# Loading the second matrix of a batched product by pairs of batches, with 16 KB in one piece per partition

## The chip, the cores and the metric

One core of one Trainium2 chip. The metric is the device time of one execution in microseconds (us), the median of several. The "span" is the part of it that the profile covers, from the first recorded event to the last. Differences here are a few tenths of a microsecond, so most kernels were run five or six times in turn with the kernel before, on the same chip. The sessions used different chips (5, 10, 8 and 0), so kernels of different sessions are compared by their ratios to the kernel before.

## The reference

```python
batch, m, k, n = 16, 512, 512, 512
a: float32 [batch, k, m];  b: float32 [batch, n, k]
out = np.matmul(a.transpose(0, 2, 1), b.transpose(0, 2, 1)).astype(np.float32)
```

For each batch the product contracts over k. The kernel gives TensorE its operands with k on the partitions: a has it there when its rows are loaded, b does not and is transposed first.

## The kernel before

SyncE loads one batch of b and one of a, 1 MiB each, into four buffers each. VectorE casts b to bfloat16, TensorE transposes it (two bfloat16 values travel as one float32), VectorE copies the result out of PSUM. ScalarE casts a. TensorE multiplies in two halves of eight matmuls; VectorE copies out the first half and ScalarE the second. Stores go out by pairs of batches, 2 MiB each: five from ScalarE's queue, the last three from SyncE after the loads.

```python
LOADS = 4; OUTS = 5; LAG = 3; TAIL = 3; H = B // 2
b_v = b.rearrange("b (ni no) k -> b ni no k", no=NO)      # NO = 4: 8 KB a partition
b_sb = [sb(f"b_sb{s}", [P, NO, K], f32) for s in range(LOADS)]
b_bf = [sb(f"b_bf{s}", [P, NO, K], cdt) for s in range(2)]
bt_ps = [ps(f"bt_ps{s}", [P, KJ, NO, P], f32) for s in range(2)]
# ... (cut)
def run_sp(sp):
    for i in range(B):
        s, use = i % LOADS, i // LOADS
        if use:
            sp.wait_ge(turned, i - LOADS + 1)
        sp.dma_start(b_sb[s][:], b_v[i]).then_inc(b_in[s], 16)
        if use:
            sp.wait_ge(summed, MO * (i - LOADS) + 1)
        if i % 2 == 0 and i // 2 >= OUTS:
            sp.wait_ge(o_out[i // 2 % OUTS], 16 * (i // 2 // OUTS))
        sp.dma_start(a_sb[s][:], a_v[i]).then_inc(a_in[s], 16)
    for j in range(H - TAIL, H - 1):
        sp.wait_ge(summed, MO * (2 * j + 2) + 3)
        store(sp, j)
    sp.wait_ge(summed, MO * (B - 1) + 3)
    store(sp, H - 1, slice(0, 1))
    sp.wait_ge(last_go, 3)
    store(sp, H - 1, slice(1, 2))
# ... (cut) TensorE
with pe.Fori(0, B // 2) as _i:
    half(0, 0)
    turn(1)
    half(0, 1)
    half(1, 0)
    half(1, 1)
    turn(0)
```

## Time and profile before

| what | value | how to read it |
|---|---|---|
| time | 125.35 us, median of 3 (125.34 to 125.48) | the number to change |
| span | 123.4 us | the profile's part of the profiled run's 125.33 |
| moved | 50.33 MB in 6800 packets, 408 GB/s over the span | a packet is what a DMA engine moves in one go: 6144 of 8 KB, and 656 of 4 bytes, 16 for each of the 41 transfers, read here as signals of completion |
| TensorE, VectorE, ScalarE | 66%, 47%, 37% busy | none is near full |

The prediction shows the lines behind this. They say: the 16 DMA engines are the bound from 3 to 121 us, and compute only has to keep up.

### The profile page before, as it was taken

To read this page: it belongs to the slowest core of one execution; us is meant where nothing else is said; L and a number is where in the kernel's file an instruction comes from. 1 tells how busy PE (TensorE), PEld (TensorE's weight loads), DVE (VectorE), ACT (ScalarE), POOL (GpSimd) and SP (SyncE) were. 2 spreads that over 40 slices of the span, in tenths; PEclk is the share of its full clock that TensorE was granted. 3 is DMA by queue.
4 is the path that set the end of the run, shared out by engine and by line. 5 is a ranking of instruction groups with operands and counts; after the bars stand their busy time and mean duration, and the time that the engine had idled before them with its cause. 6 is when DMAs were issued, how large, how long until landed. Compare 5 with 4: busy or idle time off the path is not lost. (4 is left out here: it accounts for less than half of the span.)

```text
span 123.4 us, 1091 instructions
## 1 busy us (share of the span) xinstructions
PE 81.2 (66%) x392; PEld 46.8 (38%) x392; DVE 57.9 (47%) x49; ACT 45.9 (37%) x34; POOL 0.7 (1%) x6
## 2 busy tenths in 40 slices
PE   0060699949968994999499687293569949594000
PEld 0050264626445453646264453152243536243000
DVE  0125246478545936564785555073093666530000
ACT  0037606650962269066503900907107550522000
POOL 2000000000000000000000000000000000000000
PEclk9999999999999999999999999999985999999755
DMA  3999999999999999999999999999999999999991
GB/s 64 425 425 433 425 425 425 419 422 425 425 422 420 422 422 419 427 425 425 427 425 427 425 425 425 427 433 430 435 427 422 427 425 430 427 425 425 425 425 80
DMA packets 6800, 50.33 MB, mean 408 GB/s; under 512 B 656, under 2 KB 656, under 8 KB 656
## 3 DMA queue, kind: packets, MB, share of 16 engines
q1 hardware_dynamic: 5440, 39.85, 77.4%
q10 hardware_dynamic: 1360, 10.49, 20.1%
HBM read 33.55 MB, written 16.78 MB: 408 GB/s over the span
## 5 line engine op out<-in xcount | busy, mean ns | idle before, releaser
L203 PE MATMUL o_ps<-bt_sb,a_bf 128*128 128x512 bf16 x256 | 65.0, 403 | 21.7 <-PEq L181 21.3
L203 PEld LDWEIGHTS o_ps<-bt_sb,a_bf 128*128 128x128 bf16 x256 | 28.3, 115 | 52.9 <-issue 30.4
L129 ACT CAST a_bf<-a_sb 128x2048 bf16<-128x2048 f32 (+1 forms) x16 | 29.6, 1848 | 27.3 <-DMA a_sb<-in_a_dram 27.3
L138 DVE COPY o_sb<-o_ps 128x1024 f32<-128x1024 f32 x16 | 19.6, 1225 | 20.9 <-PE o_ps L203 20.9
L143 DVE CAST b_bf<-b_sb 128x2048 bf16<-128x2048 f32 x16 | 19.5, 1222 | 20.7 <-DMA b_sb<-in_b_dram 20.6
L138 ACT COPY o_sb<-o_ps 128x1024 f32<-128x1024 f32 (+1 forms) x17 | 16.4, 962 | 30.5 <-PE o_ps L203 30.5
L191 PE MATMUL bt_ps<-identity,b_bf 128*128 128x128 f32 x136 | 19.9, 291 | 9.5 <-PEq L181 9.5
L149 DVE COPY bt_sb<-bt_ps 128x1024 f32<-128x1024 f32 x16 | 19.5, 1220 | 11.1 <-PE bt_ps L191 11.1
L191 PEld LDWEIGHTS bt_ps<-identity,b_bf 128*128 128x128 f32 x136 | 19.2, 207 | 12.5 <-issue 10.6
L129 ACT ACT_TABLE_LOAD x1 | 1.3, 1283 | 8.3 <-DMA a_sb<-in_a_dram 8.3
L129 DVE CAST a_bf<-a_sb 128x1024 bf16<-128x1024 f32 x1 | 0.7, 696 | 0.4 <-DMA a_sb<-in_a_dram 0.4
L115 POOL TENSOR_SCALAR_AFFINE_SELECT identity<-identity 128x128 f32<-128x128 f32 x1 | 0.3, 294 | 0.2 <-POOL identity L113 0.2
L113 POOL MEMSET identity<- 128x128 f32 x1 | 0.2, 205 | 0.7 <-SPq L49 0.7
L247 POOL MEMSET const-bfloat16-1.0<- 128x1 bf16 x1 | 0.1, 102 | 0.0
L247 POOL MEMSET const-uint8-127<- 128x1 uint8 x1 | 0.1, 102 | 0.0
L247 POOL MEMSET const-float32-0.0<- 128x1 f32 x1 | 0.1, 99 | 0.2 <-issue 0.2
L247 POOL MEMSET const-float32-1.0<- 128x1 f32 x1 | 0.1, 99 | 0.0
## 6 DMA issues: line engine op xcount, KB each, us to landing
b_sb<-in_b_dram SPq DMA_DIRECT2D x16, 1024.0 KB, 14.7
a_sb<-in_a_dram SPq DMA_DIRECT2D x16, 1024.0 KB, 13.6
out_dram<-o_sb ACTq DMA_DIRECT2D x5, 2048.0 KB, 14.1
out_dram<-o_sb SPq DMA_DIRECT2D x2, 2048.0 KB, 13.8
out_dram<-o_sb SPq DMA_DIRECT2D x2, 1024.0 KB, 9.8
```

The source lines that it names most:

```text
L113: pool.memset(identity[:], 0.0).then_inc(id_go, 1)
L115: pool.affine_select(out=identity[:], in_=identity[:], compare_op=mybir.AluOpType.not_equal, fill=1.0, base=0, pattern=[[-1, P]], channel_ ...
L129: copy(a_bf[i % 2][:, part, :], a_sb[s][:, part, :]).then_inc(ac_go, n)
L138: copy(o_sb[i // 2 % OUTS][:, i % 2, rm, :], o_ps[h][:, p, :]).then_inc(go, 1)
L143: dve.tensor_copy(b_bf[i % 2][:], b_sb[i % LOADS][:]).then_inc(bc_go, n)
L149: dve.tensor_copy(bt_sb[i % 2][:].rearrange("p j (ni no) -> p j ni no", no=NO), bt_ps[i % 2][:].rearrange("p j no ni -> p j ni no"),).then ...
L191: last = pe.transpose(bt_ps[x][:, j, no, :], w[:, no, j, :], identity[:])
L203: last = pe.matmul(o_ps[h][:, q, :], a_r[:, rk, 2 * h + q, :], bt_h[:, rk // 2, rk % 2, :], start=(rk == 0), stop=(rk == KO - 1),)
L247: nc = _bacc.Bacc("TRN2", target_bir_lowering=False, num_devices=1)
```

## The change

b is loaded by pairs of batches: 64 partitions for each batch, eight rows (16 KB) in one piece on each partition. The eight loads of 2 MiB have three buffers. Each transpose covers both batches of the pair. The cast b, and the transposed b in PSUM, have one buffer of double size in place of two. The last cast of a, split between two engines before, is made in one piece.

```diff
-    b_v = b.rearrange("b (ni no) k -> b ni no k", no=NO)
+    b_v = b.rearrange("(p g) (ni r) k -> p (g ni) r k", g=2, r=NR)    # NR = 8
+    PAIRS = 3
-        b_sb = [sb(f"b_sb{s}", [P, NO, K], f32) for s in range(LOADS)]
+        b_sb = [sb(f"b_sb{s}", [P, NR, K], f32) for s in range(PAIRS)]
-        b_bf = [sb(f"b_bf{s}", [P, NO, K], cdt) for s in range(2)]
+        b_bf = sb("b_bf", [P, NR, K], cdt)
-        bt_ps = [ps(f"bt_ps{s}", [P, KJ, NO, P], f32) for s in range(2)]
+        bt_ps = ps("bt_ps", [P, KJ, NR, P], f32)
 ... (cut) SyncE
+                for p in ([0] if i == 0 else [(i + 1) // 2] if i % 2 and i + 1 < B else []):
+                    if p >= PAIRS:
+                        sp.wait_ge(turned, p - PAIRS + 1)
+                    sp.dma_start(b_sb[p % PAIRS][:], b_v[p]).then_inc(b_in[p % PAIRS], 16)
-                if use:
-                    sp.wait_ge(turned, i - LOADS + 1)
-                sp.dma_start(b_sb[s][:], b_v[i]).then_inc(b_in[s], 16)
 ... (cut) ScalarE
-            copy(a_bf[i % 2][:, part, :], a_sb[s][:, part, :]).then_inc(ac_go, n)
+            act.copy(a_bf[i % 2][:], a_sb[s][:]).then_inc(ac_go, 1)
 ... (cut) TensorE
-            with pe.Fori(0, B // 2) as _i:
+            with pe.Fori(0, H) as _i:
                 half(0, 0)
+                half(0, 1)
+                take(bt_go)
+                turn(0)
+                half(1, 0)
                 turn(1)
-                half(0, 1)
-                half(1, 0)
                 half(1, 1)
-                turn(0)
```

More of the change, by code (lines that the diff above doesn't have):

```diff
@@ L25 @@
     MO = M // P
-    NO = N // P
+    NR = 2 * N // P
     assert B % 2 == 0 and B > 8
@@ L53 @@
         a_sb = [sb(f"a_sb{s}", [P, KO, M], f32) for s in range(LOADS)]
-        b_sb = [sb(f"b_sb{s}", [P, NO, K], f32) for s in range(LOADS)]
+        b_sb = [sb(f"b_sb{s}", [P, NR, K], f32) for s in range(PAIRS)]
         o_sb = [sb(f"o_sb{s}", [P, 2, MO, N], f32) for s in range(OUTS)]
         a_bf = [sb(f"a_bf{s}", [P, KO, M], cdt) for s in range(2)]
-        b_bf = [sb(f"b_bf{s}", [P, NO, K], cdt) for s in range(2)]
+        b_bf = sb("b_bf", [P, NR, K], cdt)
         bt_sb = [sb(f"bt_sb{s}", [P, KJ, N], f32) for s in range(2)]
         identity = sb("identity", [P, P], f32)
-        bt_ps = [ps(f"bt_ps{s}", [P, KJ, NO, P], f32) for s in range(2)]
+        bt_ps = ps("bt_ps", [P, KJ, NR, P], f32)
         o_ps = [ps(f"o_ps{s}", [P, MO // 2, N], f32) for s in range(2)]
         a_in = [sem(f"a_in{s}") for s in range(LOADS)]
-        b_in = [sem(f"b_in{s}") for s in range(LOADS)]
+        b_in = [sem(f"b_in{s}") for s in range(PAIRS)]
         o_out = [sem(f"o_out{s}") for s in range(OUTS)]
@@ L123, in run_pool, with cast_a @@
             ).then_inc(id_go, 1)
-        def cast_a(eng, i, part, n):
+        def cast_a(act, i):
             s = i % LOADS
-            eng.wait_ge(a_in[s], 16 * (i // LOADS + 1))
-            copy = eng.copy if eng is nc.scalar else eng.tensor_copy
-            copy(a_bf[i % 2][:, part, :], a_sb[s][:, part, :]).then_inc(ac_go, n)
+            act.wait_ge(a_in[s], 16 * (i // LOADS + 1))
+            act.copy(a_bf[i % 2][:], a_sb[s][:]).then_inc(ac_go, 1)
         def copy_out(eng, i, rm, go):
@@ L140, in run_dve, with cast_b, turn @@
         def run_dve(dve):
-            def cast_b(i, n=1):
-                dve.wait_ge(b_in[i % LOADS], 16 * (i // LOADS + 1))
-                dve.tensor_copy(b_bf[i % 2][:], b_sb[i % LOADS][:]).then_inc(bc_go, n)
-            def turn(i):
-                dve.wait_ge(turned, i + 1)
+            def cast_b(p, h):
+                n = 3 if h and p + 1 == H else 1
+                r = slice(h * NR // 2, (h + 1) * NR // 2)
+                dve.wait_ge(b_in[p % PAIRS], 16 * (p // PAIRS + 1))
+                dve.tensor_copy(b_bf[:, r, :], b_sb[p % PAIRS][:, r, :]).then_inc(bc_go, n)
+            def turn(p, g):
+                if g == 0:
+                    dve.wait_ge(turned, p + 1)
                 dve.tensor_copy(
-                    bt_sb[i % 2][:].rearrange("p j (ni no) -> p j ni no", no=NO),
-                    bt_ps[i % 2][:].rearrange("p j no ni -> p j ni no"),
+                    bt_sb[g][:].rearrange("p j (ni r) -> p j ni r", r=NR),
+                    bt_ps[:].rearrange("p j r (g ni) -> p g j ni r", g=2)[:, g],
                 ).then_inc(bt_go, 1)
-            cast_b(0)
-            cast_b(1)
-            turn(0)
-            for i in range(B - 1):
-                copy_out(dve, i, slice(0, 2), od_go)
-                turn(i + 1)
-                if i + 2 < B:
-                    cast_b(i + 2, n=1 if i + 3 < B else 2)
-            cast_a(dve, B - 1, slice(KO // 2, KO), 1)
+            cast_b(0, 0)
+            cast_b(0, 1)
+            turn(0, 0)
+            for p in range(H):
+                if p + 1 < H:
+                    cast_b(p + 1, 0)
+                copy_out(dve, 2 * p, slice(0, 2), od_go)
+                turn(p, 1)
+                if p + 1 < H:
+                    cast_b(p + 1, 1)
+                    copy_out(dve, 2 * p + 1, slice(0, 2), od_go)
+                    turn(p + 1, 0)
             copy_out(dve, B - 1, slice(0, 2), last_go)
         def run_act(act):
-            cast_a(act, 0, slice(None), 2)
-            for i in range(B - 2):
-                cast_a(act, i + 1, slice(None), 2)
+            cast_a(act, 0)
+            for i in range(B - 1):
+                cast_a(act, i + 1)
                 copy_out(act, i, slice(2, 4), oa_go)
@@ L173, in run_act @@
                     store(act, j)
-            cast_a(act, B - 1, slice(0, KO // 2), 1)
-            copy_out(act, B - 2, slice(2, 4), oa_go)
             copy_out(act, B - 1, 2, last_go)
@@ L181, in take, with turn @@
                 pe.wait_ge(s, n).then_inc(s, -n)
-            def turn(x):
+            def turn(h):
                 take(bc_go)
-                w = b_bf[x][:].bitcast(f32).rearrange("p no (pk j) -> p no j pk", j=KJ)
+                w = b_bf[:].bitcast(f32).rearrange("p r (pk j) -> p r j pk", j=KJ)
                 for j in range(KJ):
-                    for no in range(NO):
-                        last = pe.transpose(bt_ps[x][:, j, no, :], w[:, no, j, :], identity[:])
-                last.then_inc(turned, 1)
+                    for r in range(h * NR // 2, (h + 1) * NR // 2):
+                        last = pe.transpose(bt_ps[:, j, r, :], w[:, r, j, :], identity[:])
+                if h:
+                    last.then_inc(turned, 1)
             def half(x, h):
@@ L197, in half @@
                 if h == 0:
-                    take(bt_go)
-                    take(ac_go, 2)
+                    if x == 0:
+                        take(bt_go)
+                    take(ac_go)
                 take((od_go, oa_go)[h])
@@ L213, in run_pe @@
             turn(0)
-            with pe.Fori(0, B // 2) as _i:
+            turn(1)
+            with pe.Fori(0, H) as _i:
                 half(0, 0)
+                half(0, 1)
+                take(bt_go)
+                turn(0)
+                half(1, 0)
                 turn(1)
-                half(0, 1)
-                half(1, 0)
                 half(1, 1)
-                turn(0)
         run_sp(nc.sync)
```

## The prediction

> **What bounds the kernel now.** I read the page's strip of 40 slices first, because it shows whether one resource is full from end to end. The rows are tenths busy, or GB/s for the last.
>
> ```profile
> PE   0060699949968994999499687293569949594000
> ...
> DVE  0125246478545936564785555073093666530000
> ACT  0037606650962269066503900907107550522000
> ...
> DMA  3999999999999999999999999999999999999991
> GB/s 64 425 425 433 425 425 425 419 422 425 425 422 420 422 422 419 427 425 425 427 425 427 425 425 425 427 433 430 435 427 422 427 425 430 427 425 425 425 425 80
> DMA packets 6800, 50.33 MB, mean 408 GB/s; under 512 B 656, under 2 KB 656, under 8 KB 656
> ```
>
> See that every compute engine has holes, and that the DMA engines have none between the first slice and the last: 425 GB/s, whatever the others do. The 50.33 MB are 16 x 3 arrays of 1 MiB, which no kernel for this task can avoid; at 0.425 MB per us they take 118.4 us of the span's 123.4. The other 5.0 us must be start and end, so I next cut both finely in the view of windows (columns: stretch, length, busy us of PE, PEld, DVE, ACT, POOL with counts, PE clock, DMA share, GB/s).
>
> ```profile
> 1.00:2.00 1.00, 0.00 (x0) 0.00 (x0) 0.00 (x0) 0.00 (x0) 0.50 (x2) 1.00 0.31 41
> 2.00:3.00 1.00, 0.00 (x0) 0.00 (x0) 0.00 (x0) 0.00 (x0) 0.00 (x0) 1.00 0.85 156
> 3.00:4.00 1.00, 0.00 (x0) 0.00 (x0) 0.00 (x0) 0.00 (x0) 0.00 (x0) 1.00 0.93 393
> ...
> 120.00:121.00 1.00, 0.00 (x0) 0.00 (x0) 0.00 (x0) 0.00 (x0) 0.00 (x0) 0.50 0.85 360
> 121.00:122.00 1.00, 0.00 (x0) 0.00 (x0) 0.00 (x0) 0.00 (x0) 0.00 (x0) 0.50 0.04 16
> ```
>
> The transfers reach their rate at about 3 us and stop at 121: a start of some 2.6 us lost and an end of some 2.4 us. No compute engine works after 113 us, so the end is transfers only. The chain of waits that the page gives is no guide here: it ends at a tensor transpose nobody uses and holds 4% of the span.
>
> So only three things can change the time: the rate while transfers flow, the two ends, and a hole in the flow. For holes I read the load issues of SyncE and VectorE's and TensorE's loop in the timeline.
>
> ```profile
> 38.71 0.33 SPq L99 DMA_DIRECT2D a_sb<-in_a_dram  x1
> 56.60 0.33 SPq L99 DMA_DIRECT2D a_sb<-in_a_dram  x1
> ```
>
> ```profile
> 26.25 1.99 PE L203 MATMUL o_ps<-bt_sb,a_bf 128*128 128x512 bf16 x8 [1.71 <-PEq L181]
> 28.08 1.11 PE L191 MATMUL bt_ps<-identity,b_bf 128*128 128x128 f32 x8
> 29.02 5.92 PE L203 MATMUL o_ps<-bt_sb,a_bf 128*128 128x512 bf16 x24
> 34.78 1.11 PE L191 MATMUL bt_ps<-identity,b_bf 128*128 128x128 f32 x8
> 37.60 1.99 PE L203 MATMUL o_ps<-bt_sb,a_bf 128*128 128x512 bf16 x8 [1.71 <-PEq L181]
> ```
>
> One turn of the loop (two batches) takes 37.60 - 26.25 = 11.35 us, of which 1.71 us TensorE waits for VectorE to bring the transposed b out of PSUM. Two batches' loads are 4.19 MB, 9.9 us at 0.425. Until the first store (42.39 us) compute is thus a little slower than the loads, and the transfers live on a backlog. When the load at 38.71 (a of batch 8) is issued, 17 loads of 1.049 MB (17.83 MB) have been issued and 0.20 + 0.425 x (38.71 - 3.09) = 15.34 MB landed: 2.5 MB, or 5.9 us, in hand. At 56.60, after a wait for a store, 26.2 MB are issued and 22.9 landed: 3.3 MB in hand. It never runs dry, but this cushion is the thing a change could break.
>
> **What the Trainium skill says.** (1) Perfetto Trace Analysis, section What "DMA-bound" means, splits the bound into the DMA engines, the sequencer that issues, and SBUF, and says that large descriptors matter for the first two. Here it is the engines: an issue takes 0.33 us and there are 41. (2) DMA: Bandwidth & Descriptors, section Where 436 GB/s comes from, gives a ceiling of 435.2 GB/s over 16 ports; the trace's 425 agrees, 2.4% under it. (3) The same page, section Why small descriptors are slow, gives about 3 cycles a packet: 3.5 ns at its 850 MHz. The trace's packet records show a median of 309 ns for 8192 bytes; at the ceiling it would be 8192 / 27.2 = 301 ns, so up to 8 ns are overhead here, more than the page has, if it is overhead per packet at all and not simply the rate. (4) SBUF — State Buffer, section The DMA setup-cost knee, gives a 1 MiB transfer some 330-340 GB/s and a larger one more. The trace doesn't agree for this kernel: it has 425 with 1 MiB loads, because several are queued and the fixed cost of one lies under the bytes of the others. So the doubled size of the b loads should not buy what that curve suggests.
>
> **The change, part by part.**
>
> Loads of b. The 16 loads of 1 MiB become 8 of 2 MiB. Bytes are the same, and each transfer still spans 128 partitions. Packets: 128 x 16 of 8 KB become 128 x 8 of 16 KB, so 1024 fewer, 64 on each of the 16 engines; and 8 fewer completion packets per engine, 9 ns each in the packet records. Worth 8 x 9 = 0.07 us certainly, plus 64 x 8 = 0.51 us if the whole 8 ns are per packet, 64 x 3.5 = 0.22 us by the page's 3 cycles, 0 if they are rate. I choose 0.25, so -0.3 us in all (an estimate).
>
> The start. b of the first pair is complete after 2 MiB, about 8.3 us (when the second transfer landed before) in place of 5.8. Two casts of 1.22 us back to back, 16 cold transposes (8 took 1.95 us), one PSUM copy of 1.22: first product at about 8.3 + 2.4 + 2.9 + 1.2 + some waits = 15 us, before 13.55. All of it is under transfers: +0 on the end.
>
> The loop. The counts of transposes (16 a pair, 0.94 us for 8), products (4 halves of 1.83 us start to start), casts and copies stay. The order changes. With 0 at the first half: its copy on VectorE runs 2.0 to 3.2, the second turn 3.2 to 4.4, so TensorE, free at 3.7, starts the next transposes at about 4.8; then half (5.7), transposes (7.5), half (8.5 to 10.3). Meanwhile VectorE copies out 7.7 to 8.9 and turns 8.9 to 10.1, and the next pair starts at about 10.5. So the turn falls from 11.35 to about 10.5 us: the 1.71 us wait goes, a wait of about 1.1 comes. ScalarE has 2 x (1.90 + 1.01) = 5.8 us in it. Worth nothing on the end by itself, but it releases the a buffers no later.
>
> The backlog. At the start 10 MiB can be issued, not 8, as b has 6 MB of buffers, not 4. The first product at 15 plus 2 turns of 10.5 puts the issue for batch 8 at about 37; 18.87 MB are then issued and 14.6 landed: 4.3 MB in hand, against 2.5. The first store comes at about 41. So no hole in the first stage. Later, loads wait for stores as before, with 1 MiB more ahead.
>
> The end. Last loads, stores 0 to 4 landed (33.55 + 10.49 MB at 106.3 us), then stores 5, 6 and 7, 6.29 MB or 14.8 us. The last store was issued 5.8 us after the last load. The one-piece cast takes 1.90 in place of 1.05 us, and eight transposes, 0.94 us, now stand between the last batch's halves: 7.6 us. It must be there before the 5.24 MB in front of it are through, 12.3 us. Hidden: +0.
>
> Sum: 125.35 - 0.3 + 0 + 0 + 0 = 125.05 us.
>
> **The rivals.** (a) A hole in the flow: PSUM for the transposes and the cast b have one buffer now, so the pair's second turn and the next pair's transposes lock step. If the turn came to 12.5 us, the cushion would shrink by some 2 x 1.2 us up to the first store: from 10 us to 8, still none. For a loss of 2% (2.5 us) the turn would have to be near 18 us. VectorE's 7.3 us per pair speak against it. (b) Large transfers really move faster: b is a third of the bytes, and if those ran at the ceiling of 435 it would save 16.78 x (1/0.425 - 1/0.435) = 0.9 us: 124.4. The full queue speaks against it, and it is the most there is. (c) Larger b packets take turns with the stores of the other queue and starve them, so loads that wait for a store come later: the store of 14.1 us takes perhaps 20. The engines are full meanwhile, and the next store is already queued; 125.1. (d) The end grows: if the last load landed with less behind it, the longer tail of 1.8 us would show; at most 127, but 4.7 us of slack speak against it.
>
> **Range and chances.** Before, three runs lie within 0.14 us. Sure savings of 0.07, at most 0.9; the start's ramp can vary by 0.2 or 0.3 with the size of the first packets. That gives 124.5 to 125.6, most of it below the time before. Faster by over 2% needs 122.84, under what the bytes allow at the ceiling with the two ends (115.7 + 5.0 + 1.95 between span and time = 122.6, barely): 0.01. Slower by over 2% needs a hole of 2.5 us: 0.02.
>
> **What would show it.** DMA tenths of 9 in all inner slices, and packets near 5650 where 6800 were. Loop turn near 10.5 us; first product at 15; last transfer done at 120.7. A slice under 400 GB/s before the last is a hole and makes me wrong; the view of SyncE's waits would name it. A time near 124.4 would mean rate (b).

## The result, and the profile after

The changed kernel took 125.06 us (median of 4, 124.86 to 125.23), the kernel before 125.34 in the same rounds (125.16 to 125.48). The ratio is 0.9978, with a 95% interval of 0.9957 to 0.9999. A ratio is the mean time of one kernel's runs over that of the other's of the same rounds, so it is not quite the ratio of the medians. The verdict is "same", 0.28 us less; the prediction had 0.3 less.

The strip of the page of the changed kernel, the same rows as before:

```profile
PE   0007497997999799769932599965992679979600
...
DVE  0025377469295665907049007780719306162100
...
DMA  4999999999999999999999999999999999999993
GB/s 96 389 399 453 407 426 461 434 383 461 426 391 461 426 341 431 429 431 439 437 407 426 445 429 415 429 423 434 463 397 431 423 426 426 429 426 431 426 421 130
DMA packets 5648, 50.33 MB, mean 409 GB/s; under 512 B 528, under 2 KB 528, under 8 KB 528
```

The engines are still full throughout, with 1152 packets fewer: 1024 of data and 128 of completion. The GB/s row now jumps, with values of 341 to 399 in the inner slices. That looks like holes, but the DMA row stays at 9. Both rows count a packet whole in the slice where it starts, and one packet on each of 16 engines is now 262 KB, or 85 GB/s of a 3.08 us slice, so a set of packets that starts just over a boundary moves that much to the next slice. The packet records settle it: from 3 to 119 us the idle time of the engines, counted as packets in flight short of 16, adds up to 0.04 us an engine (0.00 before). Only the 341 is partly real: the records show packets taking longer between 40 and 48 us, 0.40 us an engine in all over the median, where the kernel before had 0.18.

The view of windows of the changed kernel (columns as in the prediction):

```profile
1.00:2.00 1.00, 0.00 (x0) 0.00 (x0) 0.00 (x0) 1.00 (x1) 0.50 (x2) 1.00 0.26 66
2.00:3.00 1.00, 0.00 (x0) 0.00 (x0) 0.00 (x0) 0.18 (x1) 0.00 (x0) 1.00 1.17 213
3.00:4.00 1.00, 0.00 (x0) 0.00 (x0) 0.00 (x0) 0.00 (x0) 0.00 (x0) 1.00 0.72 279
...
120.00:121.00 1.00, 0.00 (x0) 0.00 (x0) 0.00 (x0) 0.00 (x0) 0.00 (x0) 0.50 0.91 385
121.00:122.00 1.00, 0.00 (x0) 0.00 (x0) 0.00 (x0) 0.00 (x0) 0.00 (x0) 0.50 0.04 16
```

The ramp is as long as before, and transfers stop at the same place within the grain of this view. The gain must be looked for in the packets. Their records, an engine's average, read out of the trace:

| term | before | changed | difference |
|---|---|---|---|
| data packets at their median (384 x 309 ns; 256 x 309 + 64 x 611 ns) | 118.66 us | 118.21 us | -0.45 |
| time of data packets over their median | 1.34 us | 1.57 us | +0.23 |
| of that, in the first 10 us | 0.73 us | 0.88 us | +0.15 |
| completion packets | 0.38 us | 0.30 us | -0.08 |
| first data to last data, measured | 119.95 us | 119.60 us | -0.35 |

A 16 KB packet takes 611 ns, two of 8 KB take 618. The differences of the first, second and fourth row (the third is part of the second) add up to -0.30, near the measured -0.35. These are two single profiles: in the last row after_again and its five variants with 16 KB packets and nothing added (two_pairs, two_queues, split_cast, tail_4, no_idle_turns) have 119.26 to 120.05 us, and late_end_4_before 119.96.

SyncE's issues of a for batches 8 and 10 and TensorE's loop, in the timeline of the changed kernel:

```profile
37.54 0.33 SPq L103 DMA_DIRECT2D a_sb<-in_a_dram  x1
54.73 0.33 SPq L103 DMA_DIRECT2D a_sb<-in_a_dram  x1
```

```profile
30.58 1.20 PE L201 MATMUL bt_ps<-identity,b_bf 128*128 128x128 f32 x8 [0.87 <-PEq L190]
31.61 1.98 PE L215 MATMUL o_ps<-bt_sb,a_bf 128*128 128x512 bf16 x8
33.44 1.11 PE L201 MATMUL bt_ps<-identity,b_bf 128*128 128x128 f32 x8
34.38 5.85 PE L215 MATMUL o_ps<-bt_sb,a_bf 128*128 128x512 bf16 x24
41.11 1.20 PE L201 MATMUL bt_ps<-identity,b_bf 128*128 128x128 f32 x8 [0.87 <-PEq L190]
```

A turn of the loop takes 41.11 - 30.58 = 10.53 us, with one wait of 0.87 us for the copy of the second transposed b. TensorE's stall of 1.71 us is gone, and nothing came of it but an earlier issue of the loads.

Later, the loads wait longer for stores. From the view of SyncE's own waits (who waited for whom: us in total, times, longest), first the kernel before, then the changed one:

```profile
SPq L98 <- DMA out_dram<-o_sb: 26.7, 3, 9.0
```

```profile
SPq L102 <- DMA out_dram<-o_sb: 33.5, 3, 11.8
```

And the end moved. ScalarE's cast of a of batch 13, which waits for the load to land, before and changed:

```profile
92.69 1.90 ACT L129 CAST a_bf<-a_sb 128x2048 bf16<-128x2048 f32 x1 [5.81 <-DMA a_sb<-in_a_dram]
```

```profile
96.91 1.90 ACT L132 CAST a_bf<-a_sb 128x2048 bf16<-128x2048 f32 x1 [6.69 <-DMA a_sb<-in_a_dram]
```

The load of this a now stands behind the whole of the last pair's b, 2 MiB that stood behind it before. At 0.425 MB per us they take 4.9 us (an estimate), and the cast starts 4.2 us later. It is also issued later, at 72.11 us in place of 68.82, and no run separates the two. From that cast on TensorE works almost without a break to its end, which in the changed kernel reads

```profile
110.01 1.20 PE L201 MATMUL bt_ps<-identity,b_bf 128*128 128x128 f32 x8 [0.88 <-PEq L190]
111.05 1.99 PE L215 MATMUL o_ps<-bt_sb,a_bf 128*128 128x512 bf16 x8
112.88 1.11 PE L201 MATMUL bt_ps<-identity,b_bf 128*128 128x128 f32 x8
113.82 1.99 PE L215 MATMUL o_ps<-bt_sb,a_bf 128*128 128x512 bf16 x8
```

Both groups of transposes belong to a pair that doesn't exist; the loop makes them all the same. The last store was issued at 112.1 us before and at 116.5 now, and its landing took 4.7 us in place of 9.4: the end has lost most of its slack.

One thing lies outside the profile. Time minus span is 1.91 us on average in the kernel before (11 runs of a later session, spans given to a tenth), and 1.75 to 1.78 in the changed one (4 and 6 runs). So about 0.14 us of the gain is in a part that no view shows; no_idle_turns comes back to it.

### The profile page after: what moved, and what is told of

Same layout as the page of the kernel before. It is cut to its first block, busy times and chain, and to the rows that moved or that the text cites. A ratio compares the mean times of both kernels' runs of the same rounds, so it can differ in the third digit from the quotient of the medians.

```text
span 123.1 us, 1084 instructions
## 1 busy us (share of the span) xinstructions
PE 85.9 (70%) x400; PEld 49.6 (40%) x400; DVE 56.4 (46%) x48; ACT 46.8 (38%) x34; POOL 0.7 (1%) x6
## 5 line engine op out<-in xcount | busy, mean ns | idle before, releaser
L132 ACT CAST a_bf<-a_sb 128x2048 bf16<-128x2048 f32 x16 | 30.4, 1901 | 40.5 <-DMA a_sb<-in_a_dram 40.5
L201 PE MATMUL bt_ps<-identity,b_bf 128*128 128x128 f32 x144 | 24.1, 322 | 22.2 <-PEq L190 22.2
L201 PEld LDWEIGHTS bt_ps<-identity,b_bf 128*128 128x128 f32 x144 | 22.2, 212 | 27.6 <-issue 26.6
## 6 DMA issues: line engine op xcount, KB each, us to landing
out_dram<-o_sb ACTq DMA_DIRECT2D x5, 2048.0 KB, 15.2
```

The source lines that it names most:

```text
L132: act.copy(a_bf[i % 2][:], a_sb[s][:]).then_inc(ac_go, 1)
L201: last = pe.transpose(bt_ps[:, j, r, :], w[:, r, j, :], identity[:])
```

## The experiments

Theory: the transfers are the bound, so the change is worth what it saves in packets, and everything on the compute engines is hidden. Rivals: the gain is due to the order and depth of the loads; or the late end eats part of it.

**after_again.** The changed kernel as it is, as measure for the next three.

> The changed kernel once more, as the measure for the three beside it. Both theories: 0.28 us below before (ratio 0.998), 5648 packets, b packets of 16 KB at a median of 611 ns against 309 ns for 8 KB.

124.77 us (124.64 to 124.91) against 125.21 of before: ratio 0.9961, interval 0.9945 to 0.9976. The mean span fell from 123.32 to 123.00, the rest is the 0.13 us outside it. The medians differ by 0.44 us where 0.28 was expected. The two sessions differ by 0.17% in ratio, with overlapping intervals; that is the grain of what follows. In this profile the last store was issued at 117.2 us, and the DMA row has a gap that the first profile had not:

```profile
DMA  4999999999999999999999999999999999999894
```

In the packet records the engines' idle time between 110 and 119 us is 0.54 us an engine, against 0.00 in the first profile.

**packets_8k.** The same load in 8 KB packets.

```diff
-b_sb = [sb(f"b_sb{s}", [P, NR, K], f32) for s in range(PAIRS)]
+b_sb = [sb(f"b_sb{s}", [P, 2, NR // 2 * K + 8], f32) for s in range(PAIRS)]
-sp.dma_start(b_sb[p % PAIRS][:], b_v[p])
+sp.dma_start(b_sb[p % PAIRS][:, :, 0:NR // 2 * K], b_v[p].rearrange("p (h r) k -> p h (r k)", h=2))
```

> The changed kernel, with eight floats of padding between the two halves of each b row group in SBUF, so that the same 2 MiB load goes in 8 KB packets again (6672 in all). Packet theory: a 16 KB packet took 611 ns and two of 8 KB take 2 x 309 = 618, so 64 packets more on each engine cost 64 x 7 = 0.45 us: 0.45 us over the changed kernel, some 0.1 to 0.2 us over before. Rival, that the order of loads, the deeper buffers or the fewer completions brought the gain: as the changed kernel, within 0.1 us.

125.69 us (ratio 1.0037), 0.92 over the changed kernel beside it: the gain is gone, and more. The expected 0.45 is half of it. The first issue, changed kernel and then this one:

```profile
0.95 0.39 SPq L96 DMA_DIRECT2D b_sb<-in_b_dram  x1
```

```profile
0.96 0.64 SPq L96 DMA_DIRECT2D b_sb<-in_b_dram  x1
```

The load with a gap in its destination takes longer to issue, and the packet records have the first data 0.41 us later (2.37 against 1.96 us). 0.45 + 0.41 = 0.86 of the 0.92. This sum is not exact: from first to last data the profile has 119.95 us, only 0.20 to 0.35 over the changed kernel's two, and it too has a gap near the end (0.32 us an engine):

```profile
DMA  2899999999999999999999999999999999999893
```

The order of loads, the buffers and the completions are those of the changed kernel, so the first rival falls.

**packets_2k.** Padding after every row: the number of packets as a dose.

```diff
-b_sb = [sb(f"b_sb{s}", [P, NR, K], f32) for s in range(PAIRS)]
+b_sb = [sb(f"b_sb{s}", [P, NR, K + 8], f32) for s in range(PAIRS)]
-sp.dma_start(b_sb[p % PAIRS][:], b_v[p])
+sp.dma_start(b_sb[p % PAIRS][:, :, 0:K], b_v[p])
```

> The same with padding after every row of b, so packets of 2 KB: 512 for b on each engine in place of 64. Packet theory with 7 ns a packet: 448 x 7 = 3.1 us over the changed kernel, about 128.2 us. With the 3.5 ns of the skill's page: 1.6 us, 126.6. Rival (rate is rate): no change.

129.04 us (128.70 to 129.20), ratio 1.0301. The pages of the two padded kernels:

```profile
DMA packets 6673, 50.33 MB, mean 406 GB/s; under 512 B 529, under 2 KB 529, under 8 KB 529
```

```profile
DMA packets 12816, 50.33 MB, mean 396 GB/s; under 512 B 528, under 2 KB 528, under 8 KB 8720
```

The padded pair differs only in packets, apart from the pattern that the casts read (1.22 us each in both): 129.04 - 125.69 = 3.35 us for 384 more on each engine (512 for 128), 8.7 ns each. The packet records agree: 84 ns for 2 KB, so (4 x 84 - 309) / 3 = 9 ns a packet there, against 618 - 611 = 7 ns between 8 and 16 KB. So the cost is per packet.

**halves_8k.** Packets of 8 KB without padding, each half of a pair's b a load of its own.

```diff
-sp.dma_start(b_sb[p % PAIRS][:], b_v[p]).then_inc(b_in[p % PAIRS], 16)
+for h in range(2):
+    r = slice(h * NR // 2, (h + 1) * NR // 2)
+    sp.dma_start(b_sb[p % PAIRS][:, r], b_v[p][:, r]).then_inc(b_in[p % PAIRS][h], 16)
```

> The changed kernel with each 2 MiB load of b cut into two of 1 MiB, four rows (8 KB) to a partition each, one after the other with a semaphore of its own. This undoes the packet size alone, without the padding and its longer first issue (0.64 against 0.39 us), and lets the first cast start at 5.8 us, not 8.6. Packet theory: 64 x 7 to 9 ns + 8 completions x 9 ns = 0.5 to 0.65 us over the changed kernel, so about the time before (ratio 0.999 to 1.002). Rival, that the late end is what costs: this kernel computes earlier, so it would not be slower than the changed kernel (0.997).

125.53 us, ratio 1.0021 (1.0008 to 1.0034), at the upper edge of what was expected. With the changed kernel's two ratios, 0.9961 and 0.9978, that is 0.0043 to 0.0060, or 0.54 to 0.75 us over it. 0.52 of it would be packets and completions. The profile also has a stretch at 116 us with 238 GB/s, which is the late end again. A first cast at 6.1 us in place of 8.6 did not help.

**two_pairs.** `PAIRS = 2` in place of 3.

> The changed kernel with two buffers for pairs of b, 4 MB as before the change, not 6. My theory: the backlog still never runs dry (about 2 MB in hand at the thinnest by the same working), so the time stays within 0.15 us of the changed kernel and every inner slice stays full. Rival, that the deeper b buffers are what keeps the flow full: a hole in the first 45 us and 0.5 us or more over.

124.71 us, ratio 0.9965, beside 0.9961 of the changed kernel: the third buffer of 2 MiB does nothing for the time.

**split_cast.** The last cast of a split again.

```diff
+cast_a(dve, B - 1, slice(KO // 2, KO), 1)
-cast_a(act, i + 1)
+cast_a(act, i + 1) if i + 2 < B else cast_a(act, i + 1, slice(0, KO // 2), 1)
-take(ac_go)
+take(ac_go, 2)
```

> The changed kernel with the last cast of a split between ScalarE and VectorE again, with two tokens: that part of the change undone. My theory: TensorE works through from 95.5 us to 115.8 without waiting for that cast, and transfers end the span anyway: within 0.1 us of the changed kernel. Rival, that the longer cast shows at the end: up to 0.85 us faster.

125.20 us against 125.34: ratio 0.9994 (0.9981 to 1.0007), not faster than the changed kernel. By the ratios it is 0.20 to 0.41 us slower, more than the 0.1 expected, and its interval does not touch that of after_again. Its time outside the span is 1.90 us, as in the kernel before, where the changed kernel has 1.75 to 1.78: so 0.12 to 0.15 of the difference lie there. Its mean span is 0.13 us under that of before in the same rounds, after_again's 0.32; whether that is more than scatter stays open.

**late_end_2, late_end_4, late_end_4_before.** Two and four idle copies in the changed kernel, four in the kernel before, to measure the slack of the last store.

```diff
+act.wait_ge(summed, MO * (B - 1) + 4)
+for s in range(n):                       # n = 2 or 4
+    act.copy(spare[s][:], o_ps[1][:])
 copy_out(act, B - 1, 3, last_go)
```

> The changed kernel with two idle copies (0.91 us each start to start) before the last copy out, so the last store is issued 1.8 us later. In its trace the last store is issued at 116.5 and lands 4.7 us later, of which its own bytes take 2.5[...], so some 0.8 us of slack: 1.0 us over the changed kernel, about 126.1. By the prediction's step (4.7 us of slack): no change.

> The same with four idle copies, 3.6 us later. With 0.8 us of slack: 2.8 us over the changed kernel, about 127.9. By the prediction's step (4.7 us of slack): no change.

> The kernel before with the same four idle copies at its end. Its last store was issued at 112.1 and landed 9.4 us later, 4.7 us more than in the changed kernel, so by the same reckoning it has some 5.5 us of slack: no change, 125.3. If it slows as the changed kernel does, the slack is not what tells them apart.

| kernel | last store delayed by | time | ratio |
|---|---|---|---|
| late_end_2 | 1.8 us | 125.65 us (125.09 to 126.11) | 1.0022 |
| late_end_4 | 3.6 us | 126.91 us (125.85 to 127.30) | 1.0117 |
| late_end_4_before | 3.6 us | 125.35 us (125.17 to 125.68) | 1.0001 |

Against the changed kernel's 0.9961 to 0.9978 the delays of 1.8 and 3.6 us cost 0.55 to 0.76 us and 1.7 to 2.0 us. So the slack of the last store is some 1.0 to 1.9 us, varying from run to run: more than the 0.8 I had expected, far less than the 4.7 of the prediction. The kernel before has more than 3.6. (My 0.8 took off 1.4 us for the start and end of a store, which nothing had measured.) The waits of SyncE agree: where the last store came late enough to stand alone, in both late_end runs, SyncE waited 3.0 us for it after the issue; in the changed kernel's two profiles 4.8 and 4.0, in the kernel before 9.4. That leaves 1.8, 1.0 and 6.4 us. The windows of late_end_4, then of late_end_4_before:

```profile
118.00:119.00 1.00, 0.00 (x0) 0.00 (x0) 0.00 (x0) 1.00 (x2) 0.00 (x0) 1.00 0.32 131
119.00:120.00 1.00, 0.00 (x0) 0.00 (x0) 0.00 (x0) 1.00 (x2) 0.00 (x0) 0.60 0.00 0
120.00:121.00 1.00, 0.00 (x0) 0.00 (x0) 0.00 (x0) 0.04 (x1) 0.00 (x0) 0.50 0.24 98
```

```profile
118.00:119.00 1.00, 0.00 (x0) 0.00 (x0) 0.00 (x0) 0.00 (x0) 0.00 (x0) 0.50 1.03 434
119.00:120.00 1.00, 0.00 (x0) 0.00 (x0) 0.00 (x0) 0.00 (x0) 0.00 (x0) 0.50 1.05 442
```

In the first the engines stand idle until the last store comes; in the second they still have other stores to move.

**tail_4.** `TAIL = 4` in place of 3: one more store kept back behind the loads.

> The changed kernel with four stores of pairs kept back behind the loads instead of three. Loads then land up to 4.9 us earlier and 2.1 MB more lie behind the last one. Theory that the end ran out of slack in some runs (a slice of 357 GB/s near the end in the second profile): the dip goes, 0.1 to 0.4 us under the changed kernel. Rival, that the dip cost nothing or a hole opens in the middle: no gain, or slower.

124.75 us, ratio 0.9958 (0.9945 to 0.9971): no gain that can be told from the changed kernel. Its last store was issued no earlier, at 117.6 us, as a of batch 13 still came at 97.5; and its profile shows a dip too, the largest: 0.97 us an engine between 110 and 119 us. This profiled run took 125.24 us, the four others 124.68 to 124.83. The store that was kept back had not stood before that load in the first place.

**two_queues.** The first load of a issued by ScalarE.

```diff
+act.dma_start(a_sb[0][:], a_v[0]).then_inc(a_in[0], 16)     # first in run_act
+if i:                                                       # in run_sp
     sp.dma_start(a_sb[s][:], a_v[i]).then_inc(a_in[s], 16)
```

> The changed kernel with the first load of a issued by ScalarE's queue, beside the first of b on SyncE's. The first packets took up to 0.95 us per engine more than the median. If two queues overlap that, up to 0.4 us under the changed kernel; if the ramp is the memory's own, no change within 0.15 us.

124.81 us, ratio 0.9972 (0.9952 to 0.9991): no change. After 12 us from the first data it had moved 4.69 MB, as the changed kernel had (4.69 and 4.67 in its two profiles); the kernel before had moved 4.78. In the first 10 us its packets were over their median by only 0.47 us an engine in place of 0.88 and 0.95, but the engines had more idle time instead (0.63 us in the 12, against 0.23 and 0.21). So the slow start, as bytes count it, is not due to the one queue.

**no_idle_turns.** The last turn of the loop peeled off, without the two useless groups of transposes.

```diff
-with pe.Fori(0, H) as _i:
+with pe.Fori(0, H - 1) as _i:
     ...
+half(0, 0); half(0, 1); take(bt_go); half(1, 0); half(1, 1)
```

> The changed kernel with the last turn of TensorE's loop peeled off, without its two groups of eight transposes, whose results nobody uses and which stand before and between the last batch's halves. They take 2 x 0.94 us there. Theory that the end is out of slack: the last store is issued 1.5 to 2 us sooner (about 115 where the two profiles of the changed kernel have 116.5 and 117.6), no slice before the last under 400 GB/s, 0.1 to 0.4 us under the changed kernel (ratio to before near 0.995). Rival, that packets and bytes alone set the time: the store sooner, the time the same within 0.1 us (0.996 to 0.998).

125.18 us (125.11 to 125.26) against 125.16: ratio 0.9999. The last store was issued at 115.4 (after_again: 117.2; the 117.6 of the expectation is a misreading), and the strip shows no gap at the end:

```profile
DMA  5899999999999999999999999999999999999992
```

But the mean span, 122.98 us, is 0.26 under that of before in the same rounds, where after_again's was 0.32 under, so the gap seen there cost nothing on average that these runs can resolve. Single runs hint that it can cost: the profiled run with a gap was the slowest of its kernel in tail_4 and halves_8k and tied for it in after_again, the one without a gap was the fastest in the first session of the changed kernel, split_cast and two_pairs (0.07 us), but only the second of six in two_queues and the fourth of five here. One profile of each kernel does not prove it.

The time went up because the part outside the span grew to 2.21 us. The packet records hold a hint. This profile has, 1.06 us after the end of the span, a packet of the kind "instruction": 16 KB, 0.93 us. The kernel before and split_cast have one of 8 KB there (0.49 and 0.51 us), late_end_4_before one of 8 KB at 119.65 us, the ten other profiles none so late. Their times outside the span are 2.21, 1.91, 1.90 and 1.89 us, and 1.75 to 1.80 without it. So the part outside goes with a late fetch of instructions; no run tests whether that is the cause.

No version here is clearly faster than the changed kernel; two_pairs equals it with 16 KB less of SBUF on each partition.

## Why the prediction was right

**The bound: right.** The DMA row is full before and after. No run shows the faster loop or the delayed first product to have moved the time. Of the one-piece cast this can't be said: with the split one back the time was 0.20 to 0.41 us longer, in part outside the span.

**Loads of b: right in kind, the term too small.** The step chose 0.25 us out of 0 to 0.51 for the data packets. The packet records give 64 x 7 ns = 0.45, and the padded kernels show that it is a cost per packet and not simply the rate, which the step had left open. The 0.07 for completions measured 0.08.

**The start: its "+0 on the end" was wrong by a little.** The work on the first product is hidden, as said (it began at 15.36 us; 15 was predicted). But the first large packets came slower than the first small ones: 0.15 us an engine in the packet records, and after 12 us some 0.09 MB (0.2 us) less had been moved. This took back about a third of the 0.53 saved. That the size of the packets is the reason is not shown: halves_8k, with 8 KB packets, had moved 4.74 MB by then, but packets_8k only 4.66.

**The loop and the backlog: right.** 10.53 us for 10.5; the issue for batch 8 at 37.5 for 37; the first store at 40.3 for 41. two_pairs shows that the deeper buffers were not needed for it.

**The end: "hidden" held for the time as far as these runs resolve it, its slack was wrong.** The step counted 7.6 us from the last load to the last store and 4.7 us of slack. From the cast of the last a, at 106.21 us and without a wait for its load, to the last store it was 10.3 us. The late_end runs put the slack at 1.0 to 1.9 us. Two things failed in it: it took the last load of a for the one that matters, where it is that of batch 13, late, as argued above, because 2 MiB of b go ahead of it (from 99.10 us, just after its cast, TensorE had one wait of 0.88 us left); and it counted one useless group of transposes on the way, not two.

**The outside: not foreseen.** About 0.14 us of the gain lie outside the span: the profile of the kernel before has a packet of instructions after its end, those of the changed kernel have none. That the sum came out at -0.28 to -0.44 against -0.3 is thus partly luck: -0.53 in packets and completions, +0.23 in slower ones, -0.14 outside, and the scatter of the runs.

**The rivals.** (a), a hole from the single buffers, did not happen. (b), a higher rate, is what happened, at half of its most, by the size of the packets and not of the transfers (packets_8k). (c) shows at most weakly: 33.5 us of waits for stores in place of 26.7, but the stores of 14.1 us took 15.2, not 20; that large packets hold them back is not shown. (d) did not show in the mean, but was much closer than told, and some single runs hint at it. The sign that was to show a hole, a slice under 400 GB/s, was a bad one: large packets alone make such slices, and the number of packets in flight is what tells.

## What to carry to other kernels

When the DMA engines are full from end to end and the bytes stay the same, work out the change in their packets first: in this kernel the number of packets saved on each engine times 7 to 9 ns was most of what there was to gain, and a loop faster by 0.8 us a turn gained nothing that could be seen. Then look at the last store: how long other transfers still cover it is a reserve that a reordering of the loads can use up without any sign in the time, and delaying it on purpose measures it. Differences of 0.2 us need the span beside the time, as the part outside the span differs by more than that between kernels.

## What the Trainium skill lacked or had wrong

- DMA: Bandwidth & Descriptors, section Why small descriptors are slow, has about 3 cycles a packet (3.5 ns, an estimate with the 850 MHz of the same page) and 32 bytes of descriptor (1.2 ns more, an estimate at 27.2 GB/s for each engine). Measured: 7 ns between 8 and 16 KB, 9 ns between 2 and 8 KB, so the cost is larger, and it counts at these sizes too. The ceiling of 435.2 GB/s in its section Where 436 GB/s comes from agrees with the rate without that cost: 8192 B in 611 - 309 = 302 ns on 16 engines is 434 GB/s. The section also has transfers between HBM and SBUF bound by HBM, at about 358 GB/s a core; here, with one core at work, they ran at 425.
- SBUF — State Buffer, section The DMA setup-cost knee, has 330-340 GB/s for a transfer of 1 MiB. With several queued, loads of 1 MiB and stores of 2 MiB together ran at 425 GB/s; loads of 2 MiB in 8 KB packets (packets_8k) gained nothing over them.
- I found on no page that a load with a gap in its destination is issued more slowly: 0.64 against 0.39 us for the first one, in 8 KB and in 2 KB packets alike, and the first data 0.41 us later (0.42 with 2 KB).
- I found on no page that time minus span differs between kernels of one task: 1.91, 1.75 to 1.80 and 2.21 us, the span being from the first to the last instruction recorded.
